# A hybrid decoder layer on one core: the attention stage's DMA transposes issued from ScalarE's queue

## The chip, the cores and the metric

The kernel runs on one core of one Trainium2 chip. The metric is the device time of one execution in microseconds (us); a kernel's time is the median of several executions. Beside these times there is one profiled execution, from which all views of the trace come.

## The reference

One layer of a hybrid decoder on 256 tokens of width 2048, all in float32. What matters here is the attention group (32 query heads, 8 key/value heads, head width 64, a window of 128 tokens) and the products around it:

```python
proj = _rmsnorm(h, attn_norm_g) @ w_in            # z, x/B/C, dt, q, k, v
y_ssm = ...                                       # chunked state-space scan, gated, normed
qh = _partial_rope(_rmsnorm(q), cos, sin)         # by head
kh = _partial_rope(_rmsnorm(k), cos, sin)
sc = einsum('bnqhrd,bnkhd->bnhrqk', qb, kb) * scale      # 128-query blocks, band of 256 keys
m  = maximum(max(sc, -1), sink)
e  = exp(sc - m)
pr = e / (sum(e, -1) + exp(sink - m))
y_att = einsum('bnhrqk,bnkhd->bnqhrd', pr, vb)
h = h + concat([y_ssm, y_att]) @ w_out
u = causal_dwconv3(_rmsnorm(h) @ w_up);  h = h + (silu(g) * u) @ w_down
h = h + sigmoid(_rmsnorm(h) @ w_ple_gate) * _rmsnorm(p @ w_ple_proj)
```

## The kernel before

**Products.** Every large product is made of slots of twelve matmuls on TensorE. A slot takes one weight tile `w` of 128 x 1024 float32 (512 KB), loaded by `load_w` (L198) from SP's queue. ScalarE casts it to the high part `wh` (L192) and VectorE subtracts to get the low part `wl` (L193); TensorE then adds hi x wh, hi x wl and lo x wh (L222 to L224) into two accumulators. There are seven `w` buffers, four pairs `wh`/`wl` and two pairs of accumulators `acc`, so ScalarE and VectorE can be at most four slots ahead of TensorE, and a load about six.

**The attention stage** (L638 to L839) runs 104 such slots: the chunks for k, for q of group 0, for v, for q of group 1, and then, in turn, output projections (`output`) and the chunks for q of groups 2 and 3. `queries`, `keys`, `scores` and `values` are hung in at fixed slots by a table (L810 to L816). TensorE's order is thus written out by hand (`manual_schedule`). The order on all other engines and queues is set by a scheduler, which places each instruction by its own estimate of times when the program is built. Each engine runs its queue strictly in order, and so does SP's queue of DMA issues; an instruction that waits holds up all that stands behind it.

**Transposes.** The stage needs q, k and the softmax's probabilities with features or keys on the partitions. `flipped` (L683) does this by the DMA engines: the float32 tile is split into 16-bit halves (`half`), a DMA transpose moves `half` to `flip` by blocks of 128 x 128, and GpSimd puts the halves together again (L689). `half` and `flip` have two buffers each. There are 22 such transposes:

- `keys`: two, large (`flip` is 128 x 16 x 128); `half` is written by GpSimd (L713).
- `queries(j)`, for groups j = 0 to 3: two each, small (128 x 8 x 128); `half` is written by GpSimd (L701), after norm and rotation.
- `scores(j, b, kvs)`: three sets for each group, all large. For a set, TensorE makes `sc` (L738); VectorE adds the band mask (`s`, L742) and takes the negated maximum `nm` (L749, L750); ScalarE does the exponentials (L753) with their sums `den`; VectorE adds the sinks and inverts (L757, L758); ScalarE, or for the first set VectorE, scales by `den` (L761, L763); ScalarE copies into `half` (L765).

`scores` of a group follows its `queries` by some 15 slots, and `values` (L769) follows `scores`. Later, the feed-forward stage has 44 small transposes of its own (L883), which this change does not touch.

Of the kernel before, what the change touches and what calls it, by code (L numbers as in the profile page):

```python
# [65 lines left out]
def hybrid_layer(  # L66
# [20 lines left out]
    nc = tc.nc  # L87
# [20 lines left out]
    def sb(pool, shape, tag, dt=F32, bufs=None):  # L108
        kw = {} if bufs is None else {"bufs": bufs}
        size = math.prod(shape[1:]) * (2 if dt in (mybir.dt.bfloat16, U16) else 4)  # L110
        tags = sizes.setdefault(pool.id, {})
        tags[tag] = max(tags.get(tag, 0), -(-size // 32) * 32 * (bufs or pool.bufs))
        return pool.tile(shape, dt, tag=tag, name=nm(tag), **kw)
# [204 lines left out]
    with xin_:  # L318
# [21 lines left out]
        for k in range(KT):  # L340
# [9 lines left out]
            n = 1 if k < 3 else KW  # L350
# [287 lines left out]
    with tc.tile_pool(name="att_s", bufs=2) as as_, tc.tile_pool(name="att", bufs=2, reuse_waits="tile") as ap_, tc.tile_pool(name="ps_sc", bufs=1, space=PSUM) as ps_sc:  # L638
# [44 lines left out]
        def flipped(dst, n, put):  # L683

            half = sb(ap_, [P, 2, n], "half", U16)
            put(half)
            flip = sb(ap_, [P, 2 * n // P, P], "flip", U16)
            nc.sync.dma_start_transpose(flip, half.rearrange("p a n -> p (a n)"))
            G.tensor_copy(dst.bitcast(U16).rearrange("p c (t a) -> p c t a", a=2), flip.rearrange("p (a c) t -> p c t a", a=2))  # L689

        def halves(t):
# [4 lines left out]
        def queries(j, acc):  # L696
            qTs[j] = []
            for b in range(NB):
                n = norm_rope(acc, b, qrope)
                qT = sb(ap_, [P, 4, P], f"qT{b}")  # L700
                flipped(qT, NC, lambda half: G.tensor_copy(half, halves(n)))  # L701
                qTs[j].append(qT)
# [3 lines left out]
        def keys(acc):  # L706
            for b in range(NB):
                n = norm_rope(acc, b, krope, kgain)

                def twice(half):  # L710
                    h5 = half.rearrange("p a (h e d) -> p a h e d", h=8, e=2)
                    for e in range(2):
                        G.tensor_copy(h5[:, :, :, e, :], halves(n).rearrange("p a (h d) -> p a h d", h=8))  # L713

                flipped(kT[:, :, b * P : (b + 1) * P], 2 * NC, twice)
# [11 lines left out]
        def scores(j, b, kvs):  # L727
# [34 lines left out]
            else:  # L762
                V.tensor_tensor(out=s, in0=s, in1=bc(den, W), op=ALU.mult)  # L763
            p = s.rearrange("p h w -> p (h w)")
            flipped(p.rearrange("p (c t) -> p c t", t=P), 2 * m * W, lambda half: S.copy(half, halves(p)))  # L765
            for kv in kvs:
                probs[j, b, kv] = [s[:, e * m + (kv - kvs[0]) * 2 :, :][:, :2].rearrange("p h (k t) -> p h k t", t=P) for e in range(2)]
# [233 lines left out]
```

## Time and profile before

| what | us |
|---|---|
| median of 3 runs | 1434.23 (1433.61 to 1436.1) |
| profiled execution | 1436.61 |
| its span (first to last instruction) | 1434.9 |
| busy: TensorE, VectorE, ScalarE, GpSimd | 1423.2, 984.1, 804.2, 286.2 |
| first and last transpose of the stage issued at | 335.5 and 557.1 |

The rows of the profile name an engine, a line of the kernel, an operation and tiles (out<-in, without buffer numbers); an arrow `<-` in brackets or in a row of waits names what ended the wait. `SPq` and `ACTq` are the queues of SP and ScalarE, whose DMA issues are not counted as busy time. A row of the timeline begins with its start in us from the span's start and its duration; rows of one kind that follow one another are merged (xN).

### The profile page before, as it was taken

How to read it: one execution, taken by the hardware profiler on the slowest of the kernel's cores; microseconds unless marked ns; L12 is line 12 of the kernel's file. 1: busy time of each engine (PE TensorE's matmuls, PEld its weight loads, DVE VectorE, ACT ScalarE, POOL GpSimd, SP SyncE). 2: the span in 40 equal slices, each digit the busy share in tenths (PEclk: the TensorE clock that was granted, in tenths of full speed). 3: DMA queues.
4: the chain of work that ended last, by engine and by line, in shares of the span. 5: the costliest groups of instructions: out<-in, count | busy, mean ns of one | idle time of the engine just before them, and what ended most of it. 6: DMA issues, size and time to landing. Idle time of an engine off the chain costs nothing.

```text
span 1434.9 us, 18092 instructions
## 1 busy us (share of the span) xinstructions
PE 1423.2 (99%) x6527; PEld 1167.3 (81%) x6527; DVE 984.1 (69%) x1242; ACT 804.2 (56%) x1101; POOL 286.2 (20%) x212
## 2 busy tenths in 40 slices
PE   9999999999999999999999999999999999999998
PEld 7887888888787778888888888888888888888887
DVE  6678876776678897656667646765675576476854
ACT  6675555644567666556556446545554554455643
POOL 0002010008345432013243112201320131120000
PEclk9999999999999999999999999999999999999999
DMA  9656656548687778577887767867876877776671
GB/s 332 236 173 198 215 177 185 171 148 223 188 220 187 209 220 220 168 211 207 219 226 202 217 205 206 225 196 198 230 208 192 223 201 218 206 208 190 208 226 65
DMA packets 163467, 292.62 MB, mean 204 GB/s; under 512 B 93041, under 2 KB 95921, under 8 KB 162993
## 3 DMA queue, kind: packets, MB, share of 16 engines
q1 hardware_dynamic: 162944, 290.99, 70.5%
q8 instruction: 51, 0.84, 0.2%
q10 hardware_dynamic: 432, 0.48, 0.1%
q14 instruction: 40, 0.32, 0.1%
HBM read 268.32 MB, written 2.13 MB: 188 GB/s over the span
## 4 chain that ended last, share of the span: by engine, by line
PE 68%; DVE 1%; ACT 0%; issue 0%; POOL 0%; DVEq 0%; ACTq 0%
PE acc L222 22%; PE acc L224 22%; PE acc L223 22%; PE tr L779 1%; PE tr L272 0%; PE sc L738 0%; DVE wl L193 0%; ACT s L753 0%; DVE nm L749 0%; DVE s L742 0%; ACT wh L192 0%; DVE sg L931 0%; ACT s L761 0%; DVE qkr L672 0%; DVE h L396 0%
## 5 line engine op out<-in xcount | busy, mean ns | idle before, releaser
L193 DVE TENSOR_TENSOR wl<-w,wh 128x1024 fp32r<-128x1024 f32 (+1 forms) x495 | 634.9, 1288 | 378.5 <-ACT wh L192 376.4
L192 ACT CAST wh<-w 128x1024 fp32r<-128x1024 f32 (+1 forms) x495 | 514.8, 1045 | 480.7 <-PE acc L224 431.4
L223 PE MATMUL acc<-wl,ah 128*128 128x512 f32 x1278 | 500.1, 391 | 1.5 <-DVE wl L193 1.5
L224 PE MATMUL acc<-wh,al 128*128 128x512 f32 x1278 | 499.0, 391 | 0.0
L222 PE MATMUL acc<-wh,ah 128*128 128x512 f32 x1278 | 498.3, 392 | 0.0
L223 PEld LDWEIGHTS acc<-wl,ah 128*128 128x128 f32 x1278 | 240.1, 188 | 52.3 <-DVE wl L193 2.4
L222 PEld LDWEIGHTS acc<-wh,ah 128*128 128x128 f32 x1278 | 240.1, 188 | 51.0 <-issue 1.4
L224 PEld LDWEIGHTS acc<-wh,al 128*128 128x128 f32 x1278 | 240.1, 188 | 50.1 <-issue 0.7
L224 PE MATMUL acc<-wh,gl 128*128 128x512 f32 x352 | 137.1, 390 | 0.0
L223 PE MATMUL acc<-wl,gh 128*128 128x512 f32 x352 | 137.1, 390 | 0.0
L222 PE MATMUL acc<-wh,gh 128*128 128x512 f32 x352 | 136.5, 390 | 0.0
L881 POOL COPY half<-u 128x1024 uint16<-128x1024 uint16 x44 | 62.0, 1422 | 264.3 <-ACT u L879 264.3
L222 PE MATMUL acc<-wh,yh 128*128 128x512 f32 x256 | 101.6, 397 | 0.6 <-DVE h L396 0.6
L223 PE MATMUL acc<-wl,yh 128*128 128x512 f32 x256 | 99.9, 390 | 0.0
L224 PE MATMUL acc<-wh,yl 128*128 128x512 f32 x256 | 99.7, 390 | 0.0
L884 POOL COPY uc<-flip 128x1024 uint16<-128x1024 uint16 x44 | 54.9, 1248 | 177.2 <-DMA flip<-half 174.9
L223 PEld LDWEIGHTS acc<-wl,gh 128*128 128x128 f32 x352 | 66.1, 188 | 13.7
L224 PEld LDWEIGHTS acc<-wh,gl 128*128 128x128 f32 x352 | 66.1, 188 | 13.6
L222 PEld LDWEIGHTS acc<-wh,gh 128*128 128x128 f32 x352 | 66.1, 188 | 13.6
L288 DVE SCALAR_TENSOR_TENSOR cv<-uc,fcw,cv 128x254 f32<-128x254 f32 (+1 forms) x176 | 73.2, 476 | 3.4 <-ACT cv L286 3.4
L396 DVE TENSOR_TENSOR h<-h,acc 128x512 f32<-128x512 f32 x112 | 73.0, 678 | 1.8 <-PE acc L224 1.8
L222 PEld LDWEIGHTS acc<-wh,yh 128*128 128x128 f32 x256 | 48.1, 188 | 14.6 <-issue 2.0
(239 smaller groups left out, 1129.2 us busy)
## 6 DMA issues: line engine op xcount, KB each, us to landing
w<-in_w_up_dram SPq DMA_DIRECT2D x176, 512.0 KB, 4.2
w<-in_w_in_dram SPq DMA_DIRECT2D x126, 512.0 KB, 4.2
w<-in_w_down_dram SPq DMA_DIRECT2D x88, 512.0 KB, 4.3
w<-in_w_out_dram SPq DMA_DIRECT2D x64, 512.0 KB, 4.2
w<-in_w_pg_dram SPq DMA_DIRECT2D x32, 512.0 KB, 4.3
seg<-scr SPq DMA_DIRECT2D x8, 512.0 KB, 5.0
xt<-in_xT_dram SPq DMA_DIRECT2D x16, 128.0 KB, 7.0
h<-in_x_dram SPq DMA_DIRECT2D x2, 1024.0 KB, 8.7
```

The costliest lines, as they stand in the source:

```text
L192: S.copy(hi, src)
L193: V.tensor_tensor(out=lo, in0=src, in1=hi.bitcast(F32), op=ALU.subtract)
L222: PE.matmul(acc[b], lhsT=hi, rhs=wh[:, i, :], start=(k == 0), stop=False)
L223: PE.matmul(acc[b], lhsT=hi, rhs=wl[:, i, :], start=False, stop=False)
L224: PE.matmul(acc[b], lhsT=lo, rhs=wh[:, i, :], start=False, stop=(k == total - 1 or (b == NB - 1 and k + 1 == whole)))
L288: V.scalar_tensor_tensor(out=dst[:, s:], in0=ps[:, : T - s], scalar=taps[n - 1 - s], in1=dst[:, s:], op0=ALU.mult, op1=ALU.add)
L396: V.tensor_tensor(out=hs, in0=hs, in1=acc[b], op=ALU.add)
L779: PE.matmul(v3(o[e * HD : (e + 1) * HD, kv * 2 * P : (kv + 1) * 2 * P], 2), lhsT=v[kb][:, vs], rhs=pT[e][:, :, kb, :], start=(kb == 0), st ...
L881: G.tensor_copy(half.rearrange("p (a n) -> p a n", a=2), u_.bitcast(U16).rearrange("p (n a) -> p a n", a=2))
L884: G.tensor_copy(uc[:, :, b * P : (b + 1) * P].bitcast(U16).rearrange("p f (t a) -> p f t a", a=2), flip.rearrange("p (a f) t -> p f t a", ...
```

## The change

The DMA transposes of `flipped` are issued from ScalarE's queue, no longer from SP's, the queue of the weight loads. Nothing else in the code differs.

```diff
             flip = sb(ap_, [P, 2 * n // P, P], "flip", U16)
-            nc.sync.dma_start_transpose(flip, half.rearrange("p a n -> p (a n)"))
+            nc.scalar.dma_start_transpose(flip, half.rearrange("p a n -> p (a n)"))
             G.tensor_copy(dst.bitcast(U16).rearrange("p c (t a) -> p c t a", a=2), flip.rearrange("p (a c) t -> p c t a", a=2))
```

Since the scheduler places instructions anew, the order moves on several engines. TensorE's is unchanged. On SP's queue the 22 transposes go and the loads stay in their order; one piece, from group 1's second set to the q transposes of group 2:

```order
 L207 DMA w_4226<-in_w_in_dram 128x1024
-L688 DMA_TRANSPOSE flip_3842<-half_3840 128x16x128
 L207 DMA w_4244<-in_w_in_dram 128x1024
-L688 DMA_TRANSPOSE flip_3883<-half_3881 128x8x128
 L207 DMA w_4291<-in_w_in_dram 128x1024
 L207 DMA w_4309<-in_w_in_dram 128x1024
```

Loads that stood behind these two transposes no longer do. On ScalarE, at the same place (in the profile of before from 442 to 462 us), the queue was, where `s_770` is group 1's second set, `s_817` its third and the casts are those of single weight tiles:

```order
L761 ACTIVATE s_770_3816<-s_770_3816,den_3826 128x256 x4
L192 CAST wh_4059<-w_4058 128x1024
L765 COPY half_3840<-s_770_3816 128x2048
L192 CAST wh_4081<-w_4080 128x1024
L192 CAST wh_4099<-w_4098 128x1024
L192 CAST wh_4121<-w_4120 128x1024
L753 ACTIVATE s_817_3989,den_3999<-s_817_3989,nm_3996 128x256 x4
L192 CAST wh_4139<-w_4138 128x1024
L756 ACTIVATE es_4004<-es_4004 128x4
L192 CAST wh_4157<-w_4156 128x1024
L761 ACTIVATE s_817_3989<-s_817_3989,den_3999 128x256 x4
```

and it is now:

```order
L192 CAST wh_4059<-w_4058 128x1024
L761 ACTIVATE s_770_3816<-s_770_3816,den_3826 128x256 x4
L192 CAST wh_4081<-w_4080 128x1024
L765 COPY half_3840<-s_770_3816 128x2048
L688 DMA_TRANSPOSE flip_3842<-half_3840 128x16x128
L753 ACTIVATE s_817_3989,den_3999<-s_817_3989,nm_3996 128x256 x4
L756 ACTIVATE es_4004<-es_4004 128x4
L192 CAST wh_4099<-w_4098 128x1024
L192 CAST wh_4121<-w_4120 128x1024
L688 DMA_TRANSPOSE flip_3883<-half_3881 128x8x128
L761 ACTIVATE s_817_3989<-s_817_3989,den_3999 128x256 x4
```

A large transpose stands directly ahead of the third set's exponentials and a small one ahead of its scaling, and two casts that preceded the exponentials follow them. `flip_3759`, of group 1's first set, stands a little earlier, with three instructions between it and the scaling of `s_770`. On VectorE the subtractions that belong to these two casts moved behind the denominator of the same set; its queue was

```order
L749 TENSOR_REDUCE nm_3996<-s_817_3989 128x4
L396 TENSOR_TENSOR h_2_84<-h_2_84,acc_813_3970 128x512
L193 TENSOR_TENSOR wl_4100<-w_4098,wh_4099 128x1024
L750 TENSOR_TENSOR nm_3996<-nm_3996,nsink_2652 128x4
L193 TENSOR_TENSOR wl_4122<-w_4120,wh_4121 128x1024
L396 TENSOR_TENSOR h_1_83<-h_1_83,acc_827_4038 128x512
L755 TENSOR_TENSOR es_4004<-nm_3996,rows_139 128x4
```

and is now

```order
L749 TENSOR_REDUCE nm_3996<-s_817_3989 128x4
L396 TENSOR_TENSOR h_2_84<-h_2_84,acc_813_3970 128x512
L750 TENSOR_TENSOR nm_3996<-nm_3996,nsink_2652 128x4
L755 TENSOR_TENSOR es_4004<-nm_3996,rows_139 128x4
L396 TENSOR_TENSOR h_1_83<-h_1_83,acc_827_4038 128x512
L396 TENSOR_TENSOR h_2_84<-h_2_84,acc_828_4039 128x512
L757 TENSOR_TENSOR den_3999<-den_3999,es_4004 128x4
L758 RECIPROCAL den_3999<-den_3999 128x4
L193 TENSOR_TENSOR wl_4100<-w_4098,wh_4099 128x1024
L193 TENSOR_TENSOR wl_4122<-w_4120,wh_4121 128x1024
```

so `wl_4100` now waits, over the denominator, for the exponentials. The second place is group 2's third set (`s_915`; from 488 to 512 us in the profile of before). ScalarE's queue, which had `half_4286`, three casts and then the exponentials, is now:

```order
L192 CAST wh_4523<-w_4522 128x1024
L765 COPY half_4286<-s_870_4262 128x2048
L688 DMA_TRANSPOSE flip_4288<-half_4286 128x16x128
L192 CAST wh_4545<-w_4544 128x1024
L192 CAST wh_4563<-w_4562 128x1024
L753 ACTIVATE s_915_4433,den_4443<-s_915_4433,nm_4440 128x256 x4
L688 DMA_TRANSPOSE flip_4347<-half_4345 128x8x128
L756 ACTIVATE es_4448<-es_4448 128x4
L192 CAST wh_4585<-w_4584 128x1024
L761 ACTIVATE s_915_4433<-s_915_4433,den_4443 128x256 x4
```

A large transpose stands two casts ahead of the exponentials, and a small one between them and the scaling; the cast `wh_4603`, which was ahead of the scaling, follows it.

## The prediction

> **What bounds the kernel now.** I read the busy times of the page first, then the busy times by stretch, then what each engine waited for in the attention stage, and last the chain of waits around its tightest place.
>
> ```profile
> PE 1423.2 (99%) x6527; PEld 1167.3 (81%) x6527; DVE 984.1 (69%) x1242; ACT 804.2 (56%) x1101; POOL 286.2 (20%) x212
> ...
> 335.00:371.00 36.00, 35.58 (x157) 29.13 (x156) 21.25 (x20) 17.12 (x19) 22.40 (x19) 1.00 0.88 226
> 371.00:562.00 191.00, 188.22 (x919) 148.09 (x920) 159.38 (x200) 134.97 (x263) 74.90 (x55) 1.00 0.76 202
> ```
>
> The columns of the last two rows are the stretch, its length, and the busy time of TensorE (PE), its weight loads, VectorE (DVE), ScalarE (ACT) and GpSimd (POOL). TensorE is busy for 99% of the span: whatever is done elsewhere counts only where TensorE stops for it. From 335 us, where the first transpose is issued, to 562 us, after the last, it stops for 0.42 + 2.78 = 3.2 us. That is the most the change could win there. Within 371 to 562 us ScalarE is busy for 135.0 of 191 us and VectorE for 159.4. Both prepare each weight tile (ACT casts `wh`, DVE subtracts `wl`) and both run the softmax, so how late they may be is the next question:
>
> ```profile
> ACT s L753 <- DVE nm L750: 23.9, 10, 5.6
> ACT wh L192 <- PE acc L224: 14.3, 10, 3.0
> ACT s L761 <- DVE den L758: 11.6, 5, 2.8
> ...
> PE sc L738 <- POOL qT L689: 2.6, 2, 1.4
> PE acc L222 <- DVE h L396: 0.6, 1, 0.6
> ```
>
> The first three rows are ScalarE's waits in 371 to 562 us (total, times, longest). Only the middle one is slack: there ScalarE has filled all four `wh` buffers and waits until TensorE frees one, 14.3 us in all. In 35.5 us of the other two it sits in front of a softmax step that VectorE hasn't prepared. The last two rows are all that TensorE's matmuls waited for in 335 to 562 us. The chain of waits shows the tightest place:
>
> ```profile
> 442.75 1.29 ACT s L761 x3
> 444.05 0.95 ACT wh L192
> ...
> 446.16 1.29 DVE qkr L672 x2
> 447.45 1.14 DVE s L742
> ...
> 449.63 0.68 DVE h L396
> 450.31 1.13 DVE nm L749
> 451.44 0.60 DVE h L396
> ...
> 452.09 0.50 PE acc L222
> ```
>
> Up to 452.09 us the chain runs over ScalarE and VectorE, not TensorE: here the four tiles of lead are used up, and a late ScalarE makes a late end.
>
> **The transposes, as SP issues them.** Before the change 22 are issued in the stage:
>
> ```profile
> L688 SPq DMA_TRANSPOSE flip<-half x22: 1237/2734/4943, 335.5 to 557.1; - x22
> ...
> 410.80 0.33 SPq L207 DMA_DIRECT2D w<-in_w_out_dram  x1
> 411.24 4.91 SPq L688 DMA_TRANSPOSE flip<-half  x1
> ...
> 450.48 0.53 SPq L207 DMA_DIRECT2D w<-in_w_in_dram  x1
> 451.12 3.45 SPq L688 DMA_TRANSPOSE flip<-half  x1
> ...
> 495.13 2.24 SPq L688 DMA_TRANSPOSE flip<-half  x1
> 498.50 3.42 SPq L207 DMA_DIRECT2D w<-in_w_out_dram  x2
> 502.01 1.24 SPq L688 DMA_TRANSPOSE flip<-half  x1
> ...
> 542.15 0.33 SPq L207 DMA_DIRECT2D w<-in_w_out_dram  x1
> 544.61 1.64 SPq L688 DMA_TRANSPOSE flip<-half  x1
> ...
> flip<-half SPq DMA_TRANSPOSE x66, 5.5
> ```
>
> The durations (least, median, most, in ns) are time in which the issuing queue can do nothing else. The small kind (q, 8 blocks) takes 1.24 us, and once, at 451.12 us behind a load and a large transpose, 3.45; the large kind (k and the softmax sets, 16 blocks) takes 1.64 us when the last load was issued 2.4 us earlier, and 4.91 us when a load was issued 0.44 us earlier. So a large one pays for a load that stands ahead of it in its own queue.
>
> **What the change removes.** SP loses these issues, and the loads behind them may start sooner. Cost and gain: nothing. SP issues a load when `wl` has freed its buffer,
>
> ```profile
> SPq L207 <- DVE wl L193: 79.3, 30, 8.6
> ...
> w<-in_w_out_dram SPq DMA_DIRECT2D x64, 512.0 KB, 4.2
> ```
>
> for which it waits 79.3 us in 371 to 562 us; the load lands 4.2 us after issue, and no ScalarE wait for a load is among the waits of that stretch. If this cover went (loads slowed by transposes in a second queue), casts would be late next; seven `w` buffers, at most six products ahead, stand before that.
>
> **What it adds.** ScalarE's queue gets the issues. Four (two k, two q of group 0) fall before or at 371 us, where it is busy for only 17.1 of 36 us; I cost them at nothing, covered by that idle time, and `wh` would be late next if it were used up. In 371 to 562 us stand 18: 6 small and 12 large. The small ones cost 6 x 1.24 = 7.4 us. Nothing in the trace issues one from ScalarE, so the price of a large one is bounded by 1.64 and 4.91 us; I take 2.24, the row with no load within the 2 us ahead, since ScalarE's own queue holds no loads then, but the loads still use the same 16 DMA engines: 12 x 2.24 = 26.9. Sum 34.3 us (27.1 to 66.3). Page "DMA: Bandwidth & Descriptors" of the Trainium skill, section "Queues, rings and completion order", says that each DMA engine takes turns between the queues' rings, packet by packet; by this no load stands ahead of a transpose, the price would be the 1.64, and the sum below 0.4 us instead of 4.6. The two prices at 411 and 544 us agree as to loads ahead; what happens with a second queue no run here shows yet.
>
> **What hides it.** First the 14.3 us. Second, the waits for VectorE, but only where a transpose stands just ahead of one. In the new order of ScalarE's queue (shown above at two places) that is so at eight places. These are the waits of before at the instructions behind them:
>
> ```profile
> 391.98 0.51 ACT L753 ACTIVATE s<-s,nm 128x256 f32<-128x256 f32 x1 [2.64 <-DVE nm L750]
> 442.34 1.71 ACT L761 ACTIVATE s<-s,den 128x256 f32<-128x256 f32 x4 [2.77 <-DVE den L758]
> 455.28 0.51 ACT L753 ACTIVATE s<-s,nm 128x256 f32<-128x256 f32 x1 [5.64 <-DVE nm L750]
> 460.84 1.71 ACT L761 ACTIVATE s<-s,den 128x256 f32<-128x256 f32 x4 [1.49 <-DVE den L758]
> 472.38 0.40 ACT L753 ACTIVATE s<-s,nm 128x128 f32<-128x128 f32 x1 [1.74 <-DVE nm L750]
> 485.55 0.51 ACT L753 ACTIVATE s<-s,nm 128x256 f32<-128x256 f32 x1 [2.48 <-DVE nm L750]
> 503.62 0.51 ACT L753 ACTIVATE s<-s,nm 128x256 f32<-128x256 f32 x1 [4.31 <-DVE nm L750]
> 509.71 1.71 ACT L761 ACTIVATE s<-s,den 128x256 f32<-128x256 f32 x4 [2.03 <-DVE den L758]
> ```
>
> Ahead of them stand, in this order, large, large (`flip_3759`), large (`flip_3842`), small (`flip_3883`), small and large together, large, large (`flip_4288`), small (`flip_4347`). Each wait hides no more than itself or the issue: 2.24 + 2.24 + 2.24 + 1.24 + 1.74 + 2.24 + 2.24 + 1.24 = 15.4 us. What is left goes to the path: 34.3 - 14.3 - 15.4 = **4.6 us**. At 1.64 us each it is 27.1 - 14.3 - 12.4 = 0.4; at 4.91, 66.3 - 14.3 - 21.3 = 30.7. What is late then is `wh`, so `wl`, so the first matmuls of a product, near 405, 455 and 510 us.
>
> **The moved order.** Softmax steps now stand ahead of casts that they followed. At 446.69 us ScalarE cast three tiles in a row and then waited 5.64 us; now the exponentials come before two of these, and VectorE's `wl` of both after the denominator. I add nothing: the wait that was there is traded for casts that are later, within the lead. GpSimd's copies move by a place or two; its 74.9 of 191 us hide that.
>
> **A new wait.** A q transpose on ScalarE must wait for GpSimd's `half`, and the casts behind it with it. For the first one of group 1 the trace has
>
> ```profile
> 398.71 1.04 POOL L701 COPY half<-qkr 128x1024 uint16<-128x1024 uint16 x1
> ```
>
> so it is ready at 399.75 us, while the cast ahead of the transpose in the new queue ran at about 404 us. I take 0.
>
> **The sum.** The profiled execution took 1436.61 us (span 1434.9 and 1.7 around it); plus 4.6 it would take 1441.2. The median of the runs shown is 1434.23, 2.4 below the profiled one; so I predict 1438.8 for the median, 0.3% above before. A measurement of this kernel can tell about 0.2%, here 2.9 us, from no change.
>
> **Rivals.**
>
> *All hidden.* If a large issue costs 1.64 us, 0.4 us is left: 1434.6. For it: the row at 544.61; against it: the DMA engines are busy for 0.76 of this stretch (the last column but one of its row). Page "DMA: Bandwidth & Descriptors" of the Trainium skill, section "Issuing engines are not separate DMA queues", says that issuing from several engines saves only sequencer time, usually small beside the transfer; by that rule this case is the likely one. The trace disagrees as to small: a median issue of 2.73 us against 5.5 us to landing.
>
> *ScalarE becomes the bound.* With the 4.91 us price, 135.0 + 66.3 us is more than the 191 us there are: plus 30.7, 1465. Against it: on SP that price was paid only right behind a load. With SP's median, 2.73, the same working gives 7.4 + 32.8 - 14.3 - 17.5 = 8.4, so 1442.6, which I count to my forecast; from about 3.5 us it is this rival.
>
> *Faster.* Transposes out of the queue of the loads land sooner. TensorE's 2.6 us of waits for `qT` go, and the 0.6 at 452 us with them: 3.2 us, 1431.0. It decides if the q transposes land more than 1.4 us, the longest of these waits, sooner. For it: GpSimd waited for landings there,
>
> ```profile
> 370.75 1.15 POOL L689 COPY qT<-flip 128x1024 uint16<-128x1024 uint16 x1 [7.14 <-DMA flip<-half]
> ```
>
> Against it: in ScalarE's queue the same transposes stand behind casts that run no sooner.
>
> **How the numbers follow.** Forecast (slower by 3 to 14 us): 0.52. All hidden (from 1 us faster to 2.9 slower): 0.37. ScalarE bound (above 14): 0.06. Faster by over 2.9: 0.05. So faster 0.05, same 0.37, slower 0.58. The forecast alone spans 1437 to 1448; with the hidden case, whose lower bound is 1433, the range is 1433 to 1448, leaving out the two small ones.
>
> **What would show it.** Right: TensorE's idle in this stage grows from 3.2 to about 8 us, in waits for `wl` or `wh` near 405, 455 and 510 us; ScalarE's wait for TensorE falls from 14.3 towards 0; transposes in ScalarE's queue take 1.2 us (small) and near 2.2 (large). The price is wrong if large ones take 1.6 or over 3.5 us. The hiding is wrong if the softmax waits for VectorE stay as long as they were and TensorE's waits grow by more than 5 us, or if TensorE's idle doesn't grow though 34 us of issue were added.

## The result, and the profile after

| | before | after |
|---|---|---|
| median of four executions (lowest to highest) | 1434.23 (1433.61 to 1436.1) | 1449.58 (1446.98 to 1452.93) |
| profiled execution, its span | 1436.61, 1434.9 | 1451.5, 1449.8 |

The kernel became slower by a factor of 1.0106 (95% interval 1.0080 to 1.0133), some 15 us. The busy times of the page, and those by stretch for the two stretches of the prediction, after the change (columns as there: the stretch, its length, PE, PEld, DVE, ACT, POOL, granted clock, DMA share, GB/s):

```profile
PE 1430.3 (99%) x6527; PEld 1169.5 (81%) x6527; DVE 988.4 (68%) x1242; ACT 803.9 (55%) x1101; POOL 277.7 (19%) x212
...
335.00:371.00 36.00, 34.57 (x160) 28.41 (x160) 23.20 (x20) 18.09 (x21) 20.01 (x16) 1.00 0.83 219
371.00:562.00 191.00, 180.42 (x847) 138.36 (x845) 144.68 (x182) 122.05 (x242) 64.18 (x53) 0.96 0.80 183
```

Two things changed for TensorE. It stops for 1.43 + 10.58 = 12.0 us where it stopped for 3.2. And its granted clock, 1.00 in the whole stage before, is 0.96 in the long stretch: TensorE was busy *longer* than before over the whole span (1430.3 against 1423.2 us) with the same 6527 matmuls. What TensorE waited for in 335 to 562 us (total, times, longest):

```profile
PE acc L223 <- DVE wl L193: 3.9, 4, 1.9
PE acc L222 <- DVE h L396: 3.5, 2, 2.8
PE acc L222 <- ACT wh L192: 3.0, 1, 3.0
PE sc L738 <- POOL qT L689: 1.4, 1, 1.4
```

The transposes, by the view of the `flip` tiles (least, median, most of the issue in ns; last row from issue to landing in us), and below it the last row of the same view of the weight tiles `w` in 335 to 562 us, first of before and then of after:

```profile
L688 ACTq DMA_TRANSPOSE flip<-half x22: 1247/2656/5498, 331.5 to 571.5; - x22
...
DMA to landing us min/median/max: 2.7/6.3/17.3
```

```profile
DMA to landing us min/median/max: 3.3/4.2/6.7
```

```profile
DMA to landing us min/median/max: 3.4/4.6/14.5
```

Before, no transpose of the stage took over 8.45 us to land. Now five take 9.98 to 17.3 us, and loads that are in flight beside them take up to 14.5 where 6.7 was the most. The first of these shows what follows. It is issued at 381.36 us; the busy times by stretch around it:

```profile
384.00:394.00 10.00, 10.00 (x48) 7.84 (x47) 9.19 (x16) 7.44 (x18) 0.00 (x0) 1.00 1.17 95
394.00:398.00 4.00, 4.00 (x20) 3.30 (x19) 0.00 (x0) 2.42 (x4) 1.59 (x1) 1.00 0.94 358
398.00:402.00 4.00, 1.18 (x5) 0.75 (x4) 1.81 (x3) 0.00 (x0) 4.00 (x4) 0.89 0.41 167
402.00:404.00 2.00, 1.98 (x5) 1.07 (x5) 2.00 (x4) 0.00 (x0) 1.86 (x5) 0.50 0.03 8
404.00:406.00 2.00, 2.00 (x7) 1.52 (x6) 2.00 (x2) 0.00 (x0) 2.00 (x2) 0.50 0.00 0
```

For ten microseconds the DMA engines look fully busy (1.17) and move 95 GB/s; when the transpose is about to be done they move 358. In the kernel before, in 383 to 390 us, just behind the issue of the same transpose, it was 276 GB/s at a share of 1.02. GpSimd does nothing in the ten microseconds (0.00): it waits for the landing. The chain of waits, for 392 to 403 us:

```profile
381.36 14.93 DMA flip<-half
...
396.41 2.14 POOL s L689
398.55 2.38 POOL rs L187 x2
```

And in the timeline, GpSimd first, then VectorE, then TensorE:

```profile
396.41 2.14 POOL L689 COPY s<-flip 128x2048 uint16<-128x2048 uint16 x1 [20.49 <-DMA flip<-half]
398.51 3.25 POOL L187 TENSOR_TENSOR rs<-rs_t,nhalf 128x8 f32<-128x8 f32 x2
...
400.19 0.69 DVE L672 TENSOR_TENSOR qkr<-qkr,rs 128x512 f32<-128x512 f32 x1 [6.46 <-POOL rs L187]
400.80 0.68 DVE L396 TENSOR_TENSOR h<-h,acc 128x512 f32<-128x512 f32 x1
...
401.63 0.76 PE L222 MATMUL acc<-wh,yh 128*128 128x512 f32 x1 [2.82 <-DVE h L396]
```

The copy out of `flip` stands on GpSimd's queue ahead of `rs`, the inverse root that the norm of the next q needs. VectorE's normalization waits for `rs`, and behind it stands the `h` addition (L396) that frees an accumulator for TensorE. So a transpose whose result nobody needs yet stops TensorE for 2.82 us, by way of two engines' queue order. The clock column then shows the second half of the price: 0.50 from 402 us on. In the clock record, half clock lasts 6.83 us there (from 401.1 us) and 6.83 us more from 462.6 us, after the second large stop:

```profile
452.79 1.89 ACT L765 COPY half<-s 128x2048 uint16<-128x2048 uint16 x1
454.75 4.35 ACTq L688 DMA_TRANSPOSE flip<-half  x1
459.15 0.51 ACT L753 ACTIVATE s<-s,nm 128x256 f32<-128x256 f32 x1 [4.47 <-DVE h L396]
...
461.23 1.98 ACT L192 CAST wh<-w 128x1024 fp32r<-128x1024 f32 x2
...
462.31 0.59 PE L222 MATMUL acc<-wh,yh 128*128 128x512 f32 x1 [2.99 <-ACT wh L192]
```

This one is of the predicted kind. ScalarE issues for 4.35 us; the 4.47 us of idleness ahead of the exponentials are this issue (the releaser named, `h`, was there before). The casts stand behind the exponentials: TensorE waits 2.99 us for `wh`, and 0.67 more for the `wl` that follows.

The path over `rs` comes a second time, behind the transpose that is issued at 491.17 us and lands 15.41 us later:

```profile
506.70 2.14 POOL L689 COPY s<-flip 128x2048 uint16<-128x2048 uint16 x1 [11.92 <-DMA flip<-half]
508.80 3.25 POOL L187 TENSOR_TENSOR rs<-rs_t,nhalf 128x8 f32<-128x8 f32 x2
```

VectorE idles 5.16 us for this `rs`, and TensorE then stops for `wl` at 511.59 and 515.39 us (0.77 and 1.89). So 5.5 us of the 12.0 follow `rs`, and 3.7 follow the issue of 4.35 us.

The sum by the two profiles: TensorE stops 12.0 - 3.2 = 8.8 us more, and 13.66 us at half clock cost half of that, 6.8. Together 15.6 us, against 14.9 between the spans.

### The profile page after: what moved, and what is told of

Same layout as the page of the kernel before. It is cut to its first block, busy times and chain, and to the rows that moved or that the text cites. A ratio compares the mean times of both kernels' runs of the same rounds, so it can differ in the third digit from the quotient of the medians.

```text
span 1449.8 us, 18080 instructions
## 1 busy us (share of the span) xinstructions
PE 1430.3 (99%) x6527; PEld 1169.5 (81%) x6527; DVE 988.4 (68%) x1242; ACT 803.9 (55%) x1101; POOL 277.7 (19%) x212
## 4 chain that ended last, share of the span: by engine, by line
PE 66%; DMA 3%; DVE 2%; POOL 1%; ACT 1%; issue 1%; ACTq 0%; DVEq 0%; POOLq 0%
PE acc L222 22%; PE acc L223 22%; PE acc L224 21%; DMA flip<-half 2%; DVE wl L193 1%; DMA w<-in_w_out_dram 1%; PE tr L779 1%; PE tr L272 0%; ACTq L688 0%; PE sc L738 0%; ACT s L753 0%; POOL s L689 0%; ACT wh L192 0%; ACT half L765 0%; DVE nm L749 0%
## 5 line engine op out<-in xcount | busy, mean ns | idle before, releaser
L223 PEld LDWEIGHTS acc<-wl,gh 128*128 128x128 f32 x352 | 66.1, 188 | 13.7
L224 PEld LDWEIGHTS acc<-wh,gl 128*128 128x128 f32 x352 | 66.1, 188 | 13.7
L396 DVE TENSOR_TENSOR h<-h,acc 128x512 f32<-128x512 f32 x112 | 73.5, 681 | 3.1 <-PE acc L224 3.0
```

Of the source, the lines that this page charges most:

```text
L223: PE.matmul(acc[b], lhsT=hi, rhs=wl[:, i, :], start=False, stop=False)
L224: PE.matmul(acc[b], lhsT=lo, rhs=wh[:, i, :], start=False, stop=(k == total - 1 or (b == NB - 1 and k + 1 == whole)))
L396: V.tensor_tensor(out=hs, in0=hs, in1=acc[b], op=ALU.add)
```

## The experiments

The theories: *late landing* (transposes in one queue and loads in another slow each other down; what stands behind the landing does the harm) against *ScalarE's issue time* (46.0 us by the timeline, six small and eleven large issues in 371 to 562 us; the twelfth large one came at 571.51), with the *new order* of the queues as a third. All ran beside the kernel before; the medians of before were 1434.05 to 1434.27.

| kernel | transposes / loads of the stage from | landings over 9 us (longest) | TensorE stops in 335 to 562 us | half clock in the stage | median, ratio to before (95%) |
|---|---|---|---|---|---|
| before | SP / SP | 0 (8.4) | 3.2 | 0 | 1434.23 |
| after | ScalarE / SP | 5 (17.3) | 12.0 | 13.7 | 1449.58, 1.0106 (1.0080 to 1.0133) |
| after_again | ScalarE / SP | 8 (17.5) | 16.8 | 17.1 | 1450.42, 1.0128 (1.0106 to 1.0151) |
| q_on_act | 8 small ScalarE, 14 large SP / SP | 0 (8.7) | 3.7 | 3.4 | 1439.68, 1.0030 (1.0020 to 1.0041) |
| sets_on_act | 12 large ScalarE, rest SP / SP | 5 (19.5) | 15.5 | 13.7 | 1451.68, 1.0118 (1.0103 to 1.0132) |
| busy_instead | SP / SP, ScalarE kept busy | 0 (8.6) | 1.8 | 0 | 1432.81, 0.9990 (0.9981 to 0.9998) |
| root_on_dve | ScalarE / SP | 7 (16.3) | 7.3 | 3.4 | 1445.12, 1.0080 (1.0064 to 1.0096) |
| halved | ScalarE / SP | 8 (12.1) | 6.6 | 3.4 | 1447.58, 1.0084 (1.0055 to 1.0113) |
| loads_on_act | SP / ScalarE | 8 (16.4) | 12.0 | 17.1 | 1452.58, 1.0120 (1.0100 to 1.0141) |
| all_on_act | ScalarE / ScalarE | 0 (7.2) | 12.6 | 20.5 | 1456.37, 1.0154 (1.0138 to 1.0169) |
| less_load | ScalarE / SP, quarter loads | 0 (4.9) | 1.9 | 0 | 1433.95, 0.9996 (0.9987 to 1.0006) |
| less_load_sp | SP / SP, quarter loads | 0 (4.5) | 0.0 | 0 | 1430.95, 0.9977 (0.9968 to 0.9986) |

Landings, stops and clock are those of each kernel's one profiled execution, the stops being 227 us less TensorE's busy time. That execution lay above the median in after_again (1458.55) and sets_on_act (1456.1), and below it in halved (1441.42) and q_on_act (1437.03). The stage also ends later in the slower kernels: after 562 us there are 3.3 us more of stops in all_on_act and 1.0 in after_again.

**busy_instead: ScalarE's time without the second queue.**

```diff
-            nc.scalar.dma_start_transpose(flip, half.rearrange("p a n -> p (a n)"))
+            nc.sync.dma_start_transpose(flip, half.rearrange("p a n -> p (a n)"))
+            h2 = half.rearrange("p a n -> p (a n)")
+            dum = sb(as_, [P, 512], "dum", U16, 1)
+            for _ in range(4):
+                S.copy(dum, h2[:, :512])
```

> All transposes are issued from SP as before; ScalarE runs four copies of 128x512 into a spare tile behind each `half` instead (about 0.55 us each, 22 x 2.2 = 48 us, where the issues of the changed kernel held it for 46 us in 371 to 562 us). Scaling: ScalarE pays, no second queue. ScalarE's issue time: as slow as the changed kernel or slower, 1446 to 1455. Late landing: landings stay at 3.7 to 8.5 us, GpSimd's waits for them near 30 us, the clock 1.0, and only the price on the path, 1435 to 1441.

The copies by their tile, then the stretch, of this kernel:

```profile
L692 ACT COPY dum<-half x88: 601/616/631, 331.3 to 559.2; 128x512 uint16<-128x512 uint16 x88
```

```profile
371.00:562.00 191.00, 190.48 (x921) 150.34 (x920) 159.44 (x200) 174.19 (x338) 71.00 (x55) 1.00 0.78 207
```

ScalarE is busy for 174.2 us instead of 135.0, and TensorE stops less than before. 39 us of work on ScalarE in this stretch cost nothing; the kernel is even 0.1% faster, which I put down to no cause. So ScalarE's time as such isn't what the change cost. The copies are short, though, 0.6 us each and mostly with casts between them; they don't imitate a single issue that holds ScalarE for 4 us or more. Late landing was right on landings and clock, but too high by 2 us, and wrong on GpSimd: its waits for landings add up to 116 us in 335 to 565 us here, as many as after the change (118.9). A total of GpSimd's waits tells nothing; what stands behind the wait does.

**Two queues or one: loads_on_act and all_on_act.** `load_w` gets its queue as an argument; in the first kernel the transposes go back to SP, in the second they stay on ScalarE.

```diff
-                products(acc, aT, load_w(w_in[c, s]), s * KW, KW, KT, s == n - 1)
+                products(acc, aT, load_w(w_in[c, s], queue=nc.scalar), s * KW, KW, KT, s == n - 1)
...
-                    products(acc, lhs, load_w(w[i0 * 2 + s, n]), s * KW, KW, KG, s == 1)
+                    products(acc, lhs, load_w(w[i0 * 2 + s, n], queue=nc.scalar), s * KW, KW, KG, s == 1)
```

> The other way round: the transposes stay in SP's queue and the attention stage's weight loads are issued from ScalarE. Two queues again, but ScalarE issues no transpose. Late landing by two queues: large transposes of over 9 us again, in SP's queue now, with loads of over 10 us beside them; the time at least that of the changed kernel, 1445 to 1475, since ScalarE also waits for w buffers. If it were something of ScalarE's queue: all landings under 9 us.

> Transposes and the attention stage's weight loads all issued from ScalarE: one queue, though not SP's. Late landing by two queues: no transpose over 9 us, as in the kernel before, whatever the time (ScalarE then waits for w buffers, 1440 to 1480). If it were ScalarE's queue as such that lands late: over 9 us again at three places or more.

The `flip` tiles of loads_on_act, then of all_on_act:

```profile
L688 SPq DMA_TRANSPOSE flip<-half x22: 1232/2745/5629, 333.4 to 572.6; - x22
...
DMA to landing us min/median/max: 2.7/6.6/16.4
```

```profile
L688 ACTq DMA_TRANSPOSE flip<-half x22: 1247/2674/5134, 336.5 to 577.0; - x22
...
DMA to landing us min/median/max: 3.7/5.1/7.2
```

Both came out as late landing had it. With before and after they make a square: two queues, whichever carries what, give landings of 16 to 17 us; one queue, whichever it is, at most 8.4. Neither is a way out. all_on_act is the slowest of all for another reason, one stop of 9.36 us for the first `qT`, whose transpose is issued at 372.48 us where it was issued at 363.60 after the change. Its `half` was ready at 365.25 us, but in the one queue the issue stands behind a load that went out only at 372.10 us.

**less_load and less_load_sp: less traffic to compete with.** Each load of the stage brings 128x256 instead of 128x1024, and both the cast and the subtraction read that quarter four times; the products are then of other weights.

```diff
-            nc.sync.dma_start(w2[:, s], src[:, s])
-            split(w2[:, s], wh2[:, s], wl2[:, s])
+            q = slice(i * n, i * n + n // part)
+            nc.sync.dma_start(w2[:, q], src[:, q])
...
+                r = [v3(t[:, s], part) for t in (wh2, wl2)]
+                split(w2[:, q].unsqueeze(1).to_broadcast([P, part, n // part]), *r)
```

> The changed kernel with a quarter of each weight load in the attention stage (128x256 in place of 128x1024; the casts and subtractions read it four times over, so that their work stays the same; the products are of other weights). The second queue, all 22 issues on ScalarE and the order of after's kind stay; the traffic they compete with falls to a quarter. Late landing through competition with the loads: large transposes land within 7 us, their issue shortens to 1.6 to 2.3 us, GpSimd's waits for flips fall under 70 us in 371 to 562 us, TensorE stops for 1 to 4 us, the clock stays 1.0: 1430 to 1437. The order of the queues, or a second queue as such: landings over 9 us or stops of 8 us or more remain, 1444 to 1451.

> The control for the quarter loads: the same quarter of each weight load (the products are of other weights), transposes issued from SP as before. The competition with the loads: with so little traffic it doesn't matter who issues, so the same time as with ScalarE's issues and a quarter of the loads (1433.95), within 2 us. If ScalarE's issues or the new order cost something of their own that the lighter loads only made up for: 1425 to 1431 here.

The `flip` tiles of less_load, then the stretch in less_load_sp:

```profile
L693 ACTq DMA_TRANSPOSE flip<-half x22: 1247/1667/2428, 331.6 to 552.8; - x22
...
DMA to landing us min/median/max: 2.7/3.9/4.9
```

```profile
371.00:562.00 191.00, 191.00 (x926) 151.15 (x925) 164.63 (x202) 136.19 (x264) 77.34 (x55) 1.00 0.34 85
```

With a quarter of the traffic the same issues on ScalarE take at most 2.43 us (5.50 after the change), all land within 4.9 us, and the kernel is as fast as before. Again GpSimd's waits (97.1 us in 371 to 562) were not the sign that I had made of them. The control shows a smaller part of its own: issued from SP, the lighter kernel takes 1430.95, so ScalarE's issues with their new order cost 3.0 us here. If the parts add, about 3 of the 15 us are ScalarE's issues and the order, and 12 the competition of two queues, with its late landings and its longer issues. The 3 hold for issues as short as here (median 1.67 us, against 2.66 after the change). The order alone wasn't separated: the copies of busy_instead give an order between the two.

**root_on_dve: the path behind the late landing.** VectorE makes a reciprocal where GpSimd made the inverse root of q's and k's norm; the root is left out.

```diff
-        G.tensor_tensor(out=r, in0=t, in1=nhalf[:, :cols], op=ALU.pow)
+        if dve:
+            V.reciprocal(r, t)
+        else:
+            G.tensor_tensor(out=r, in0=t, in1=nhalf[:, :cols], op=ALU.pow)
```

> The changed kernel, but the inverse root of q's and k's norm (L187, 10 steps of 1.65 us on GpSimd) is taken off GpSimd: VectorE makes a reciprocal in its place (the root itself is left out, so the scale of q and k differs). Late landing: transposes land as late as in the changed kernel, but VectorE no longer waits 11.6 us for rs behind GpSimd's wait; the stop of TensorE at 399 us (2.82 us, for h) and the half clock after it (3.4 us) go: 1441 to 1445. ScalarE's issue time: nothing of it changes, 1448 to 1451, and both stops stay.

VectorE's wait for `rs` in 371 to 562 us after the change, a row that is gone here, and then TensorE's waits of this kernel in 335 to 565 us:

```profile
DVE qkr L672 <- POOL rs L187: 11.6, 2, 6.5
```

```profile
PE acc L226 <- DVE wl L196: 3.0, 4, 1.5
PE acc L225 <- ACT wh L195: 1.5, 1, 1.5
PE acc L225 <- DVE h L399: 1.5, 2, 0.8
PE acc L225 <- ACT s L764: 1.2, 1, 1.2
```

Transposes landed as late as ever (16.3 us), GpSimd waited more, and yet the kernel gained 4.5 us on the change, 0.1 less than the smallest gain expected (its interval overlaps that of after and lies below that of after_again). No wait for `h` is longer than 0.8 us; at 398 us TensorE stops for 1.16 us, and the clock stays. Two new stops at 411.14 and 413.17 us (1.53 and 1.48) bring 3.41 us of half clock of their own. So the path over `rs` is real, and one of several. VectorE's wait for `rs` marks it better than GpSimd's total: 11.6 us after the change, 12.6 in after_again and 18.2 in loads_on_act, at most 0.6 in all other kernels. Among these are halved and sets_on_act, which have late landings too, so in these profiles their loss comes another way.

**q_on_act and sets_on_act: which transposes.**

```diff
-            nc.scalar.dma_start_transpose(flip, half.rearrange("p a n -> p (a n)"))
+            (nc.scalar if n == NC else nc.sync).dma_start_transpose(flip, half.rearrange("p a n -> p (a n)"))
```

In sets_on_act the condition is a flag that only `scores` gives.

> Only the 8 small transposes (q) are issued from ScalarE; the 14 large ones (k and the softmax sets) stay in the queue of the loads. Late landing (transposes in a second queue share the DMA engines with the loads and land up to 17 us late): in the changed kernel every landing over 9 us was a large one, so none here is over 9 us, TensorE stops for about 3 us in 335 to 562 us and the clock stays 1.0: 1434, within 3 us of before. ScalarE's issue time: 8 x 1.25 = 10 us, under the 14.3 us of slack: the same 1434. A third, that it is the second queue as such and not the size: landings over 9 us here too and 1440 or more.

> Only the 12 large transposes of the softmax sets are issued from ScalarE; k and q stay in the queue of the loads. Late landing: four or so land after 13 us or more, GpSimd waits over 40 us for them, VectorE's norm steps wait behind it, TensorE stops for 8 to 12 us, and each stop of 2.8 us or more is followed by 6.8 us at half clock: 1444 to 1450. ScalarE's issue time: 12 x 3.3 = 40 of the 46 us measured in all, so nearly the whole loss, 1446 to 1450, but with waits for wh and wl and none for GpSimd or landings. If the loss comes from the q transposes after all: 1434 to 1437.

The `flip` tiles of q_on_act, then of sets_on_act:

```profile
L688 ACTq DMA_TRANSPOSE flip<-half x8: 1247/1249/1330, 363.2 to 515.2; - x8
...
DMA to landing us min/median/max: 3.7/5.6/8.7
```

```profile
L688 ACTq DMA_TRANSPOSE flip<-half x12: 1631/3670/8168, 381.2 to 574.2; - x12
...
DMA to landing us min/median/max: 2.7/6.4/19.5
```

The large sets alone give the whole loss, 1.7 us beyond the range, so this pair didn't separate the theories. The trace of sets_on_act shows a second path. The issue at 416.12 us holds ScalarE for 8.17 us; ScalarE's next cast comes after 7.24 idle us, and TensorE stops for `wh` from 424.27 us (1.24) and for `wl` from 426.01 us (1.98). Here `wh` and `wl` take 12.1 of the 15.5 us. So the two queues do harm in two ways: landings come late, and the issues on ScalarE grow long. For the small ones every view was right and the time was not: 1439.68, where I expected 1434 within 3. The profiled execution, 1437.03, is one of the two fastest of nine; it has 3.41 us of half clock from 452.2 us, after stops of 1.07 and 0.69. What the slower ones had more isn't seen. So this second queue costs some 4 to 5 us with no landing over 9 us in its profile, and late landing doesn't explain that.

**halved and after_again.** halved issues a large transpose as two:

```diff
+            for a in range(2 if n > NC else 1):
+                m = n // P if n > NC else 2 * n // P
+                nc.scalar.dma_start_transpose(flip[:, a * m : (a + 1) * m], half[:, a, :] if n > NC else half.rearrange("p a n -> p (a n)"))
```

> The changed kernel with each large transpose issued as two of 8 blocks (128x8x128) from ScalarE: the same bytes and packets in the same second queue. Late landing through competition of bytes: the second of a pair still lands over 9 us after the first was issued at three places or more, 1442 to 1451. If it is the length of one transpose that matters (the small ones alone landed within 7 us): no pair over 9 us, 1434 to 1440. ScalarE's issue time would be 2 x 1.25 = 2.5 us in place of 2.7 to 5.

> The changed kernel once more, for a second profile and more executions beside the runs above. If late landing is a matter of which loads happen to be in flight, the places of the late ones shift from execution to execution but there are again three or more large ones over 9 us, TensorE stops for 8 to 13 us in 335 to 562 us, and stops that add up to about 2 us or more within 4 us bring half clock for 3.4 or 6.8 us: 1446 to 1453. If the first profile showed a chance event, no landing over 9 us and 1436 to 1441.

The `flip` tiles of halved, then of after_again:

```profile
L690 ACTq DMA_TRANSPOSE flip<-half x36: 1247/1328/5042, 331.0 to 563.9; - x36
...
DMA to landing us min/median/max: 2.7/6.0/12.1
```

```profile
L688 ACTq DMA_TRANSPOSE flip<-half x22: 1247/1852/9936, 331.1 to 579.8; - x22
...
DMA to landing us min/median/max: 2.7/6.7/17.5
```

Halving shortens the longest landing but doesn't take the loss away, so the length of one transpose isn't the whole cause; with less_load this speaks for bytes in two queues that compete. In the second profile of the change the late ones shift (two small ones are among them, 10.54 and 11.57 us), the first at 381 us is late again, and the stops are larger than I expected, 16.8 us:

```profile
398.76 2.12 POOL L689 COPY s<-flip 128x2048 uint16<-128x2048 uint16 x1 [23.06 <-DMA flip<-half]
...
403.95 0.76 PE L222 MATMUL acc<-wh,yh 128*128 128x512 f32 x1 [5.38 <-DVE h L396]
```

## Why the prediction was wrong

Slower was right, at 0.58; the time was not: 1438.8 with a range up to 1448, against 1449.58. Step by step:

- *What the change removes: "Cost and gain: nothing."* This step failed, and it is the main one. The text named the cover (loads slowed by transposes in a second queue, seven `w` buffers) and took it to be there. Loads took up to 14.5 us where 6.7 was the most, and the cover held for the loads alone; nothing covered the transposes. The stops behind the two late landings that held up `rs` make 5.5 us, and 6.83 us of half clock begin with the first of them.
- *"GpSimd's copies move by a place or two; its 74.9 of 191 us hide that."* This failed with it. A busy share hides nothing in a queue that runs in order: GpSimd was idle for 20.49 us and yet ran `rs`, whose input was there at 388.9 us, only at 398.51. The total of its waits would not have shown it either; the question to ask was what stands behind the copy.
- *The price of a large issue, 2.24 us "since ScalarE's own queue holds no loads".* Mis-sized: the eleven in 371 to 562 us took 38.2 us, 3.5 each and up to 5.01; the longest of all, at 341.79 us, took 5.50, and one of sets_on_act 8.17. The price follows what else the DMA engines carry: 2.43 at most with quarter loads. It doesn't take a load ahead in the same queue, as the text had it for the 4.91: ScalarE's queue had none when 5.50 was paid.
- *What hides it: 4.6 us to the path.* Not shown right. 39 us of plain work on ScalarE cost nothing, so more is hidden than 14.3 + 15.4 = 29.7 us, if it comes in short pieces; the issues with their order cost 3.0 us in light traffic, and one stop of 2.99 us at 459 us is of the predicted kind, as are those of sets_on_act at 424 and 426 us. "The moved order: nothing" and the new wait for `half` stay untested by themselves.
- *What would show it.* TensorE's idle grew to 12.0 instead of 8 us, and the first large stop was for `h`, at 399 us, which no step had. The other 6.9 us for `wh` and `wl` came at 459 to 524 us, so near two of the three places named, but 2.7 of them behind `rs`. ScalarE's slack fell from 14.3 to 8.1 us, not to 0; its softmax waits for VectorE fell from 35.5 to 25.6. The small issues took 1.25 us, as forecast, but for one of 1.59.
- *The clock* was in no step. It took 6.8 of the 15 us.
- *The rivals.* "All hidden" failed with its price: the large issues took 3.5 us, not 1.64. "Faster" failed at its own point: the q transposes landed 2.71 to 8.03 us after issue where it had been 4.69 to 6.14, so two of the eight came by more than 1.4 us sooner, one later by 1.9, and TensorE's waits for `qT` fell only from 2.6 to 1.4 us. "ScalarE becomes the bound" had the price from 3.5 us on and the time 1465; the price was reached and the bound was not. Page "DMA: Bandwidth & Descriptors" of the Trainium skill, section "Queues, rings and completion order", has each DMA engine take turns between rings by packets; the runs agree that both queues are slowed at once; why only 95 GB/s moved in all, they don't show.

## What to carry to other kernels

A second issuing queue is not free just because the issuing engine has time: ask what its transfers will meet in the DMA engines, and for each landing which instruction waits for it and what stands behind that one in its queue. A transfer whose result is needed much later still stops the kernel if its consumer blocks an engine that runs in order. An issue that grows long holds its engine in the same way: 39 us in short pieces cost nothing here, and behind one issue of 8.17 us TensorE stopped for 3.2. Price a stop of TensorE near 2 us or more at more than itself, since half clock may follow.

## What the runs showed of the hardware

- DMA transposes in one queue and 512 KB loads in another: landings up to 19.5 us instead of 8.4, loads up to 17.1 (sets_on_act) instead of 6.7, and 95 GB/s at a DMA share of 1.17. In those ten microseconds the transpose's 1595 packets (0.40 MB) took 73% of the DMA engines' time and the loads' 143 packets (0.54 MB) 43%, 0.48 us each; in the four after them 380 packets of the loads took 0.16 us each. In one queue, on SP or on ScalarE, no landing was late (7.2 to 8.6 at most), nor with eight small transposes alone in the second queue (8.7) or with quarter loads (4.9).
- Kernels with two such queues and full loads also vary more: 1434.27 to 1441.6 (q_on_act), 1441.26 to 1452.68 (halved); with one queue 1431.54 to 1433.73 (busy_instead) and 1455.97 to 1457.19 (all_on_act).
- In the stage, half clock came in stretches of 3.41 us or multiples of it: after single stops of 2.82, 2.99 and 5.38 us 6.83 us, after stops of 1.07 and 0.69 within 2.7 us 3.41 us; in after_again a stop of 2.48 us at 514.46 us brought none and one of 1.85 at 520.00 us 3.41. Within a run these stretches start on one grid of 3.41 us, and what seems to count is how long TensorE stands still within one interval of it: 1.67 to 3.41 us in the interval ahead of every such stretch in the eight kernels that have them, at most 1.79 in those of the stage with none behind. The 2.48 us fell into two intervals, as 1.70 and 0.78. Page "TensorE: Matmul & The Clock Gate" of the Trainium skill, section "Part 1: The HAM clock gate", gives a free-running window of about 3.4 us and an idle window as the condition; the lengths agree, but no stop of 3.4 us was needed here.
